# Float32 hybrid encoder step on one core: the blocks of the split activations move from a stride of 292 floats to 320, all starting at 32 modulo 256 bytes

## The chip, the cores and the metric

One Trainium2 chip, one of its cores. The metric is the device time of one execution in microseconds (us); the kernel before was run three times (median 2174.95 us) and once more under the hardware profiler.

## The reference

One layer of a streaming encoder for 256 prompt frames and 32 sample frames, with model width 2048, all in float32:

```python
x = x + 0.5 * swiglu(rmsnorm(x, norm_ffn1), w_ffn1_in, w_ffn1_out)   # 2048 -> 2 x 5504 -> 2048
y, state = mix(rmsnorm(x, norm_mix))   # h @ w_in, split among three head groups:
#   A: GLA linear attention, 4 heads, chunks of 64; B: differential attention, 4 heads;
#   C: cross-attention into 256 memory tokens (w_mem_kv); then concat @ w_o
x = x + y
x = x + 0.5 * swiglu(rmsnorm(x, norm_ffn2), w_ffn2_in, w_ffn2_out)
return rmsnorm(x, norm_final), state
# rmsnorm(x, g) = x * rsqrt(mean(x^2) + 1e-6) * g ; swiglu(x) = (silu(x @ gate) * (x @ up)) @ w_out
```

## The kernel before

**Layout.** Activations are kept transposed: `x_res` holds x as 16 blocks of 128 features (partitions) by NT = 288 tokens (free axis). In every large product the weights are the stationary operand of TensorE, in tiles of 128x128, and a block of 288 tokens is the moving operand; the output is a block of 128 output features by 288 tokens in PSUM.

**Split in two.** To keep float32 precision on TensorE's fast float32r path, each operand is split into a high and a low half (`split`, `gsplit`): hi is a copy rounded to float32r, lo is the rest. A product is three matmuls: weights-hi x moving-hi, weights-hi x moving-lo, weights-lo x moving-hi. The split activations are `uh`, `ul` (input of the FFNs and of the mixer, 16 blocks), `hh`, `hl` (the FFN's hidden activations, 22 blocks, named `hha`, `hhb`, ... for the two FFNs), `cdh`, `cdl` and `gch`, `gcl` (mixer outputs that go into w_o). Blocks of `uh`, `ul`, `hh`, `hl` lie NS = 292 floats apart, those of the last four NT = 288 floats apart.

**Weights.** All weights pass through one ordered list of chunks of mostly 128x1024 floats (4 k-blocks of 256 columns): a load into one of three `ws` buffers by the SP queue (L169), a split into `wh` on ScalarE (L102, the profile's ACT) and `wl` on VectorE (L90, DVE) into one of four buffers each, then the matmuls. `consume` hands out a chunk, splits three chunks ahead and loads three further. `gemm` gives a chunk 24 matmuls: first, for each of two column blocks and four k-blocks, wh with hi and wh with lo; then wl with hi. Four chunks make one output pair of 2x128 features from 16 k-blocks:

```python
                        if part == 0:
                            mm(o, wh[:, j, cs], xh, ci == 0 and j == 0, False)
                            mm(o, wh[:, j, cs], xl, False, False)
                        else:
                            mm(o, wl[:, j, cs], xh, False, ci == nchunk - 1 and j == nk - 1)
```

**Order.** The program order of each engine is written by hand: memory keys and values (w_mem_kv, where the weights are the moving operand with 512 columns and `mTh`, `mTl` the stationary one), FFN 1, mixer projection w_in, w_o, FFN 2. Between chunks `side()` takes small steps of four threads (attention heads, preparations).

**Normalisation.** The row scale R of rmsnorm is applied after the product. `prep_sq` sums squares into `acc`; `later_R` sums `acc` over the partitions with a matmul against ones and turns it into R in `rsq` (six instructions on VectorE and ScalarE); the outputs of each product are then multiplied by R through `Rb`. R has a tile of its own, R_ffn1, R_mix, R_ffn2 in one buffer. In the mixer, `glr` (16 rows x 288) is the low-rank gate input, of which the product has 16 columns only (`mglr`), and `wg2` its second weights; `mats` holds constants: a 128x128 block matrix `bones` of which only two columns are used (`bcols`), a mask `tri` and a row mask `smask`.

**Addresses.** Tiles of a pool lie behind one another in the order in which they are first used, each rounded up to 32 bytes. So in each partition `uh` starts at byte 20608 and `ul` at 39296 (both 128 modulo 256), `hh` at 150048 (32 modulo 256) and `hl` at 175744 (128). With a stride of 1168 bytes, which is 144 modulo 256, block k of `uh` and `ul` starts at 128 + 144k modulo 256, of `hh` at 32 + 144k. `cdh`, `cdl`, `gch`, `gcl` have a stride of 1152 bytes, so that their blocks start at 32 and 160 by turns. The weights buffers begin at byte 74016 and follow in steps of 4096; every 128-column block in them starts at 32 modulo 256.

Of the kernel before, what the change touches and what calls it, by code (L numbers as in the profile page):

```python
# [10 lines left out]
F32 = mybir.dt.float32  # L11
# [7 lines left out]

P = 128  # L20
NT = 288
NS = 292
D = 2048
KB = 16
NF = 43
# [9 lines left out]
G_MEM, G_F1, G_MQ, G_MIX, G_F2, G_FIN, G_BG, G_GO, G_DO, G_DQ, G_N = 0, 16, 32, 33, 49, 65, 81, 85, 87, 88, 89  # L35
# [5 lines left out]
def hybrid_step_kernel(  # L41
# [9 lines left out]
    pe, dve, act, sp = nc.tensor, nc.vector, nc.scalar, nc.sync  # L51
# [4 lines left out]
    const = pool("const")  # L56
# [10 lines left out]
    def c4(name):  # L67
        return c4p.tile([P, 1024], F32, tag="c4", name=name)
# [10 lines left out]
    def sq2(name):  # L79
        return sqp.tile([P, 2, NT], F32, tag="sq", name=name)  # L80
# [11 lines left out]
    def mul(out, a, b):  # L92
        dve.tensor_tensor(out, a, b, op=ALU.mult)  # L93
# [220 lines left out]
    ones = const.tile([P, P], F32, name="ones")  # L314
    dve.memset(ones, 1.0)
    x_res = const.tile([P, KB, NT], F32, name="x_res")
    uh = const.tile([P, KB, NS], F32R, name="uh")[:, :, :NT]
    ul = const.tile([P, KB, NS], F32R, name="ul")[:, :, :NT]
    acc = const.tile([P, NT], F32, name="acc")
    G = const.tile([P, G_N], F32, name="G")  # L320
    dkc = const.tile([P, 4, P], F32, name="dkc")
    dvc = const.tile([P, 512], F32, name="dvc")
    Bx = const.tile([P, 4, 384], F32, name="Bx")
    Bs = const.tile([P, 160], F32, name="Bs")
    lam = const.tile([P, 1], F32, name="lam")
    mkn = ft.tile([P, P], F32, name="mkn")
    gdk = const.tile([P, 64], F32, name="gdk")
    mats = const.tile([P, 544], F32, name="mats")
    bones, tri, smask = mats[:, 0:128], mats[:, 128:256], mats[:, 256:544]
    bcols = bones.rearrange("p (b c) -> p b c", c=64)[:, :, 0]  # L330

    def gcol(i):
        return G[:, i:i + 1]

    def rsq(out, src, n, rows=P, scale=1.0, tiles=None):

        w = src.shape[1]
        v, r, t = tiles or (sm(f"rs{k}")[:rows, :w] for k in range(3))
        dve.tensor_scalar(v, src, 1.0 / n, EPS, op0=ALU.mult, op1=ALU.add)
        act.activation(r, v, AF.Ln)  # L340
        act.activation(r, r, AF.Exp, scale=-0.5)
        mul(t, v, r)
        stt(t, t, -0.5 * scale, r, ALU.mult, ALU.mult)
        stt(out, t, 1.5 * scale, r, ALU.add, ALU.mult)

    def rsq_all(out, sums, v, n):

        ps = s1("sums")
        mm(ps[:, :NT], ones, sums)
        rsq(out, ps[:, :NT], n, tiles=(v, out, sums))  # L350


    T3 = (0, 128, 160)
# [20 lines left out]
        for b in (2 * i, 2 * i + 1):  # L374
            gsplit(uh[:, b, :], ul[:, b, :], x_res[:, b, :], gcol(g0 + b))

    Rt = {}

    def later_R(name):

        def f():
            R = const.tile([P, NT], F32, tag="R", name=f"R_{name}")
            rsq_all(R, acc, sq2("rw")[:, 0, :], float(D))
            fresh[0] = True
            Rt[0] = R
        t_main.add(f, f"R_{name}")

    def Rb(n):
        return Rt[0].unsqueeze(1).to_broadcast([P, n, NT])


    hp = fstack[0][1]
    mTh = hp.tile([P, 22, NS], F32R, tag="hh", name="mTh").rearrange("p a t -> p (a t)")[:, :4096]
    mTl = hp.tile([P, 22, NS], F32R, tag="hl", name="mTl").rearrange("p a t -> p (a t)")[:, :4096]
    mTh = mTh.rearrange("p (k m) -> p k m", m=256)
# [5 lines left out]
    tr(pt[:, :16], gmem)  # L401
    act.copy(G[:, :16], pt[:, :16])

# [132 lines left out]
    S = {}  # L536

    def lam_a():
        ld = S["ld"] = sq2("ld").rearrange("p a c -> p (a c)")[:, :256]
        sp.dma_start(ld, diff_lambda[0].rearrange("a d -> (a d)").unsqueeze(0).partition_broadcast(P))  # L540
        sp.dma_start(gdk, diff_k_norm.partition_broadcast(P))
        sp.dma_start(mats, c_mats[:, 128:672])

    def lam_b():
        l4 = S.pop("ld").rearrange("p (a b d) -> p a b d", a=2, b=2)
# [81 lines left out]
        dve.tensor_copy(Bx[:, :, 0:128], Bx[:, :, 256:384])  # L627

    def wg2_a():
        S["wg2"] = c4("wg2")[:16, :512]  # L630
        sp.dma_start(S["wg2"], w_gla_g2[0])

    def s0_a():
# [10 lines left out]
    def ffn(tag, mark, g_next, final=False):  # L644
# [8 lines left out]
        for half, (a, b) in enumerate(HALVES):  # L653
            hh = hp.tile([P, 22, NS], F32R, tag="hh", name=f"hh{tag}{half}")[:, :, :NT]
            hl = hp.tile([P, 22, NS], F32R, tag="hl", name=f"hl{tag}{half}")[:, :, :NT]
            f = a
# [49 lines left out]
    mxp = mstack.enter_context(tc.tile_pool(name="mxp", bufs=1))  # L706
# [16 lines left out]
        dve.memset(a, 0.0)  # L723
    dec = mxp.tile([P, 4, 5], F32, name="dec")
    junk = mxp.tile([P, P], F32, name="junk")
    glr = mxp.tile([16, NT], F32, name="glr")
    rsm = mxp.tile([P, 9], F32, name="rsm")
    rsd = mxp.tile([P, 18], F32, name="rsd")
    osum = mxp.tile([P, 18], F32, name="osum")
# [402 lines left out]
    for kind, c0, g in MIX:  # L1132
        if kind == "glr":
            ps = psm.tile([P, 2, 512], F32, tag="m", name="mglr")
            nk, (wh, wl) = consume()
            for j in range(nk):
                o = ps[:16, 0, :NT]
                mm(o, wh[:, j, :], uh[:, j, :], j == 0, False)
                mm(o, wh[:, j, :], ul[:, j, :], False, False)
                mm(o, wl[:, j, :], uh[:, j, :], False, j == nk - 1)  # L1140
            mul(glr, ps[:16, 0, :NT], Rt[0][:16, :])
            for f in (lambda: gla_z(0), lambda: gla_z(1), gla_g1, gla_g2):
                t_gla.add(f)
            t_gla.add(gla_g3, "E1")
            t_gla.add(gla_g4)
            side()
            continue
        ps = gemm(4, u)
        need("R_mix")
        pv = ps[:, :, :NT]  # L1150
        if kind in ("mq", "dq", "dk", "dv", "gk"):
            if g == 0:
                M[kind] = t4(kind)
            mul(M[kind][:, 2 * g:2 * g + 2, :], pv, Rb(2))
        if kind == "gr":
            if g % 2 == 0:
                M.setdefault("sgr", []).append(t4("sgr"))
            raw = M["sgr"][g // 2][:, 2 * (g % 2):2 * (g % 2) + 2, :]
            mul(raw, pv, Rb(2))
        elif kind == "gk" and g == 1:  # L1160
            for j in range(2):
                t_gla.add(lambda j=j: gla_k1(j))
                t_gla.add(lambda j=j: gla_k2(j), lag=1)
        elif kind == "mq" and g == 1:
            head_sums(t_mem, "mq", ones[:, 0:1], 128.0, 1, rsm, MS)
            t_mem.pipe([[(mem_a, 0), (mem_c, 2), (mem_b, 1), (mem_e, 0)], [(mem_n, 0)]], 5, "mem", lags=(1, 2))
        elif kind == "dq" and g == 1:
            head_sums(t_diff, "dq", bcols, 64.0, 2, rsd, DS)
        elif kind == "dk" and g == 1:
            t_diff.pipe([[(dk_b, 1), (dk_a, 0)]], 3)  # L1170
        elif kind == "dv" and g == 1:
            for t in range(3):
                t_diff.add(lambda t=t: dv_a(t), lag=1)
            t_diff.pipe([[(diff_a, 0), (diff_c, 2), (diff_b, 1), (diff_s, 0)], [(diff_e, 0)], [(diff_n, 0)]], 5,
                        lags=(1, 1, 2))
            t_diff.add(dv_out, lag=1)
            t_diff.add(od_a)
            for k in range(3):
                t_diff.add(lambda k=k: od_b(k), "diff" if k == 2 else None, lag=1)
        elif kind == "gq":  # L1180
            need("E1")
            raw = sq2("gqraw")
            mul(raw, pv, Rb(2))
            qe = M["GB"][:, 2 * g:2 * g + 2, :]
            stt(qe, raw, 128 ** -0.5, qe, ALU.mult, ALU.mult)
        elif kind == "gv":
            if g == 0:
                need("mem")
                need("diff")
                M["gvt"] = [c4(f"gvt{t}") for t in range(3)]  # L1190
            raw = M["gv", g] = tL("gvraw")[:, :2 * NT].rearrange("p (b t) -> p b t", t=NT)
            mul(raw, pv, Rb(2))

            def f0(g=g):
                if g:
                    gla_D(g - 1)
                gla_v(g)

            def f1(g=g):
                gla_A(g)  # L1200
                if g:
                    gla_E(g - 1)
            t_gla.add(f0, lag=1)
            if g == 0:
                for t in range(3):
                    t_gla.add(lambda t=t: gla_kdt(t), lag=1, after="diff")
                t_gla.add(silu_r, lag=0)
            t_gla.add(f1, lag=1)
            t_gla.add(lambda g=g: gla_B(g), lag=1)
            t_gla.add(lambda g=g: gla_C(g), lag=1)  # L1210
            if g == 3:
                t_gla.add(lambda: gla_D(3), delay=2)
                t_gla.add(lambda: gla_E(3), "gla")
        side()

    for half in range(2):
        if half == 1:
            need("gla")
        for g in range(8):
            if half == 0:  # L1220
                ps = gemm(2, lambda k: (cdh[:, k, :], cdl[:, k, :]))
            else:
                ps = gemm(2, lambda k: tuple(a[:, k % 4, :] for a in M["cat", k // 4]))
# [48 lines left out]
    ps = s1("yss")  # L1272
# [7 lines left out]
    for k, (hf, t, parts) in enumerate(((0, 0, 2), (0, 1, 1), (0, 2, 1), (1, 2, 1), (1, 0, 1), (1, 1, 1))):  # L1280
        rows = slice(0, P) if t < 2 else slice(96, P)
        dst = y_prompt[0, t * P:(t + 1) * P] if t < 2 else y_sample[0]
        n = 1024 // parts
# [66 lines left out]
```

## Time and profile before

| what | value |
|---|---|
| median of three runs (lowest, highest) | 2174.95 us (2172.83, 2175.52) |
| the profiled execution | 2173.12 us |
| its span, first to last instruction | 2171.3 us |
| TensorE matmuls (PE): busy, number | 2152.7 us, 16010 |
| VectorE (DVE) busy | 1116.0 us |
| ScalarE (ACT) busy | 867.2 us |
| bytes moved by DMA | 353.72 MB, mean 163 GB/s |
| granted TensorE clock, mean | 0.997 |

PE stands for TensorE's matmuls and PEld for its weight loads, which run beside the matmuls. A matmul's own duration overlaps with the next one's; the distance between two starts is what one costs. In the lists, a group is named output<-inputs by the program's tile names, with the number of instructions after the x.

### The profile page before, as it was taken

The numbers are of one execution on the slowest core, as the hardware profiler recorded it, in microseconds if no ns is written. First come the engines' busy times: TensorE is split into PE (matmuls) and PEld (weight loads), VectorE is DVE, ScalarE is ACT, GpSimd is POOL, SyncE is SP. The second block draws the span as 40 slices with busy tenths as digits, with TensorE's granted clock in tenths as the row PEclk, the third lists the DMA queues.
The fourth block names the chain that finished last, engine by engine and source line by source line (L and its number), as shares of the span: only waits on it lengthen the run. The fifth ranks groups of instructions, "written<-read, shape, count | busy, mean of one in ns | idle before, by whom it ended". The sixth has DMA issues, their size and how long they took to land.

```text
span 2171.3 us, 37498 instructions
## 1 busy us (share of the span) xinstructions
PE 2152.7 (99%) x16010; PEld 2119.4 (98%) x16010; DVE 1116.0 (51%) x1315; ACT 867.2 (40%) x1117; POOL 0.7 (0%) x6
## 2 busy tenths in 40 slices
PE   8999999999999999999999999999999999999997
PEld 6999999999999999999999899999999999999997
DVE  6754444444554455554664666554444445444453
ACT  6643333333333344433444344333333333333433
POOL 0000000000000000000000000000000000000000
PEclk9999999999999999999999999999999999999999
DMA  7556555555555545554445345555555555555453
GB/s 257 165 177 199 169 169 176 161 168 168 164 163 172 164 153 169 174 161 121 120 138 151 114 152 166 165 164 170 168 164 162 164 175 156 171 169 165 154 162 117
DMA packets 351028, 353.72 MB, mean 163 GB/s; under 512 B 13889, under 2 KB 342717, under 8 KB 350861
## 3 DMA queue, kind: packets, MB, share of 16 engines
q1 hardware_dynamic: 350860, 351.32, 53.2%
q8 instruction: 125, 2.05, 0.4%
q14 instruction: 43, 0.34, 0.0%
HBM read 345.55 MB, written 5.64 MB: 162 GB/s over the span
## 4 chain that ended last, share of the span: by engine, by line
PE 99%; DMA 0%; ACT 0%; DVE 0%; SPq 0%; ACTq 0%; issue 0%; DVEq 0%
PE m L83 92%; PE mm L83 2%; PE go L83 1%; PE xt L87 0%; PE gKo L83 0%; PE mglr L83 0%; PE do L83 0%; PE mo L83 0%; DMA mem<-in_mem_prompt_dram 0%; PE gKe L83 0%; PE msc L83 0%; PE dsc L83 0%; PE mt L87 0%; PE sums L83 0%; PE yt L87 0%; PE hs_dq L83 0%
## 5 line engine op out<-in xcount | busy, mean ns | idle before, releaser
L90 DVE TENSOR_TENSOR wl<-ws,wh 128x1024 fp32r<-128x1024 f32 (+2 forms) x665 | 781.8, 1190 | 678.6 <-ACT wh L102 648.1
L102 ACT CAST wh<-ws 128x1024 fp32r<-128x1024 f32 (+2 forms) x665 | 665.9, 1020 | 668.2 <-PE m L83 534.5
L83 PE MATMUL m<-uh,wh 128*128 128x288 f32 x3392 | 916.5, 296 | 0.0
L83 PE MATMUL m<-ul,wh 128*128 128x288 f32 x3392 | 911.1, 295 | 0.0
L83 PEld LDWEIGHTS m<-uh,wh 128*128 128x128 f32 x3392 | 638.5, 188 | 3.8 <-issue 2.9
L83 PEld LDWEIGHTS m<-ul,wh 128*128 128x128 f32 x3392 | 639.0, 188 | 0.2
L83 PE MATMUL m<-uh,wl 128*128 128x288 f32 x3392 | 517.7, 295 | 0.0
L83 PEld LDWEIGHTS m<-uh,wl 128*128 128x128 f32 x3392 | 473.5, 188 | 0.0
L83 PE MATMUL m<-hhb,wh 128*128 128x288 f32 x688 | 186.2, 296 | 0.0
L83 PE MATMUL m<-hla,wh 128*128 128x288 f32 x688 | 185.8, 296 | 0.0
L83 PE MATMUL m<-hlb,wh 128*128 128x288 f32 x688 | 185.7, 296 | 0.0
L83 PE MATMUL m<-hha,wh 128*128 128x288 f32 x688 | 185.7, 295 | 0.0
L83 PEld LDWEIGHTS m<-hlb,wh 128*128 128x128 f32 x688 | 129.9, 189 | 0.0
L83 PEld LDWEIGHTS m<-hla,wh 128*128 128x128 f32 x688 | 129.8, 189 | 0.0
L83 PEld LDWEIGHTS m<-hha,wh 128*128 128x128 f32 x688 | 129.3, 188 | 0.0
L83 PEld LDWEIGHTS m<-hhb,wh 128*128 128x128 f32 x688 | 129.3, 188 | 0.0
L83 PE MATMUL m<-hha,wl 128*128 128x288 f32 x688 | 106.7, 295 | 0.0
L83 PE MATMUL m<-hhb,wl 128*128 128x288 f32 x688 | 106.6, 295 | 0.0
L83 PEld LDWEIGHTS m<-hha,wl 128*128 128x128 f32 x688 | 96.6, 188 | 0.0
L83 PEld LDWEIGHTS m<-hhb,wl 128*128 128x128 f32 x688 | 96.6, 188 | 0.0
L665 ACT ACTIVATE gs_b<-gs_b 128x576 f32<-128x576 f32 (+1 forms) x22 | 14.8, 674 | 84.8 <-DVE gs_b L93 84.8
L102 ACT CAST hhb<-hm_b 128x576 fp32r<-128x576 f32 (+1 forms) x22 | 14.6, 663 | 83.4 <-DVE hm_b L93 83.4
(286 smaller groups left out, 1195.9 us busy)
## 6 DMA issues: line engine op xcount, KB each, us to landing
ws<-in_w_ffn_in_dram SPq DMA_DIRECT2D x336, 512.0 KB, 4.5
ws<-in_w_ffn_out_dram SPq DMA_DIRECT2D x160, 512.0 KB, 3.6
ws<-in_w_in_dram SPq DMA_DIRECT2D x80, 512.0 KB, 3.7
ws<-in_w_o_dram SPq DMA_DIRECT2D x32, 512.0 KB, 3.7
ws<-in_w_mem_kv_dram SPq DMA_DIRECT2D x16, 512.0 KB, 4.8
ws<-in_w_ffn_out_dram SPq DMA_DIRECT2D x16, 256.0 KB, 2.8
ws<-in_w_ffn_in_dram SPq DMA_DIRECT2D x16, 256.0 KB, 3.9
x<-in_x_prompt_dram SPq DMA_DIRECT2D x4, 512.0 KB, 7.3
```

The lines of the kernel that those rows point to most:

```text
L83: pe.matmul(out, lhsT, rhs, start=start, stop=stop)
L90: dve.tensor_tensor(out, a, b, op=op)
L102: act.copy(hi, src)
L665: act.activation(gs, gs, AF.Silu)
```

## The change

NS becomes 320, so that the stride is 1280 bytes, five times 256. `G` and `lam` are moved ahead of `uh`, which puts `uh` at byte 21024 and `ul` at 41504, both 32 modulo 256; with 20480 and 28160 bytes per tile, `hh` (152096) and `hl` (180256) come to 32 modulo 256 too, and so does the start of the weights buffers (76064). Each block of `uh`, `ul`, `hh`, `hl` then starts at 32 modulo 256 bytes. `mTh` and `mTl`, which use the buffers of `hh` and `hl`, do so as well.

To make room, R is written over `acc`, with the second half of the scratch tile as the temporary that `acc` was; `mats` shrinks from 544 to 442 floats by loading two columns of `bones` alone, with two DMAs in place of one; `glr` moves into the unused part of the `wg2` buffer.

```diff
-NS = 292
+NS = 320
...
     x_res = const.tile([P, KB, NT], F32, name="x_res")
+    G = const.tile([P, G_N], F32, name="G")
+    lam = const.tile([P, 1], F32, name="lam")
     uh = const.tile([P, KB, NS], F32R, name="uh")[:, :, :NT]
     ul = const.tile([P, KB, NS], F32R, name="ul")[:, :, :NT]
     acc = const.tile([P, NT], F32, name="acc")
-    G = const.tile([P, G_N], F32, name="G")
...
-    lam = const.tile([P, 1], F32, name="lam")
...
-    mats = const.tile([P, 544], F32, name="mats")
-    bones, tri, smask = mats[:, 0:128], mats[:, 128:256], mats[:, 256:544]
-    bcols = bones.rearrange("p (b c) -> p b c", c=64)[:, :, 0]
+    mats = const.tile([P, 442], F32, name="mats")
+    bcols, tri, smask = mats[:, 0:2], mats[:, 2:130], mats[:, 130:418]
...
-    def rsq_all(out, sums, v, n):
+    def rsq_all(out, sums, v, n, t=None):
...
-        rsq(out, ps[:, :NT], n, tiles=(v, out, sums))
+        rsq(out, ps[:, :NT], n, tiles=(v, out, sums if t is None else t))
...
-            R = const.tile([P, NT], F32, tag="R", name=f"R_{name}")
-            rsq_all(R, acc, sq2("rw")[:, 0, :], float(D))
+            w = sq2("rw")
+            rsq_all(acc, acc, w[:, 0, :], float(D), w[:, 1, :])
             fresh[0] = True
-            Rt[0] = R
...
     def Rb(n):
-        return Rt[0].unsqueeze(1).to_broadcast([P, n, NT])
+        return acc.unsqueeze(1).to_broadcast([P, n, NT])
...
-        sp.dma_start(mats, c_mats[:, 128:672])
+        sp.dma_start(mats[:, 0:2], c_mats[:, 191:193])
+        sp.dma_start(mats[:, 2:418], c_mats[:, 256:672])
...
-        S["wg2"] = c4("wg2")[:16, :512]
+        a = c4("wg2")
+        S["wg2"], S["glr"] = a[:16, :512], a[:16, 512:512 + NT]
...
-    glr = mxp.tile([16, NT], F32, name="glr")
+    glr = S["glr"]
...
-            mul(glr, ps[:16, 0, :NT], Rt[0][:16, :])
+            mul(glr, ps[:16, 0, :NT], acc[:16, :])
```

More of the change, by code (lines that the diff above doesn't have):

```diff
@@ L375, in prep_u @@
             gsplit(uh[:, b, :], ul[:, b, :], x_res[:, b, :], gcol(g0 + b))
-    Rt = {}
     def later_R(name):
         def f():
-            R = const.tile([P, NT], F32, tag="R", name=f"R_{name}")
-            rsq_all(R, acc, sq2("rw")[:, 0, :], float(D))
+            w = sq2("rw")
+            rsq_all(acc, acc, w[:, 0, :], float(D), w[:, 1, :])
             fresh[0] = True
-            Rt[0] = R
         t_main.add(f, f"R_{name}")
     def Rb(n):
-        return Rt[0].unsqueeze(1).to_broadcast([P, n, NT])
+        return acc.unsqueeze(1).to_broadcast([P, n, NT])
     hp = fstack[0][1]
```

## The prediction

> **What bounds the kernel now.** I read the page first (busy shares, the chain), then the chain in order of time, then the start times of single matmuls on TensorE.
>
> ```profile
> span 2171.3 us, 37498 instructions
> ...
> PE 2152.7 (99%) x16010; PEld 2119.4 (98%) x16010; DVE 1116.0 (51%) x1315; ACT 867.2 (40%) x1117; POOL 0.7 (0%) x6
> ...
> PE 99%; DMA 0%; ACT 0%; DVE 0%; SPq 0%; ACTq 0%; issue 0%; DVEq 0%
> ```
>
> TensorE is the chain: 99% of it. ACT and DVE are busy 40% and 51%, so only TensorE's own pace or a new wait on it can move the end. "Busy" says nothing about pace, since matmuls overlap (296 ns each in the groups below). The pace is the distance from one start to the next, and the chain in order of time has it:
>
> ```profile
> 29.49 5.54 PE mm L83 x24
> ...
> 294.96 601.10 PE m L83 x4536
> ...
> 1075.53 6.26 PE mglr L83 x48
> ```
>
> Columns: start, length, what, how many. 4536 matmuls of 288 columns, all in the first FFN, run without a gap in 601.10 us: 132.5 ns each. Set beside the memory stage (the first row: 512 columns, 5.54/24 = 230.8 ns), the difference is 98.3 ns over 224 columns, 0.439 ns a column; so 288 columns cost 126.4, and 6.1 ns come on top of each matmul.
>
> How many matmuls read a tile whose stride changes (`uh`, `ul`, `hh`, `hl`; the stage letters a and b stand behind the last two):
>
> ```profile
> L83 PE MATMUL m<-uh,wh 128*128 128x288 f32 x3392 | 916.5, 296 | 0.0
> ...
> L83 PE MATMUL m<-uh,wl 128*128 128x288 f32 x3392 | 517.7, 295 | 0.0
> L83 PE MATMUL m<-hhb,wh 128*128 128x288 f32 x688 | 186.2, 296 | 0.0
> ...
> L83 PE MATMUL m<-hhb,wl 128*128 128x288 f32 x688 | 106.6, 295 | 0.0
> ```
>
> Three groups of 3392 (`uh` and `ul` with wh, `uh` with wl) and six of 688 (`hh`, `hl` with wh and `hh` with wl, in two FFNs), of each the first and the last shown: 14304. (Each mean of the wl rows is 295 too; only overlap makes their busy sums small.) One ns on each of these is 14.3 us, 0.66% of the span. So a change of 0.2%, about what a measurement of this kernel can tell from no change, is 0.3 ns per matmul.
>
> **Does the start of a block matter at all, and what is it worth at 32?** The kernel before answers this by itself, because its blocks start at different places modulo 256 bytes. The gate's halves `gch`, `gcl` in the second part of w_o have blocks 1152 bytes apart, starting by turns at 32 and at 160; their order is hi, lo of block 0 (32), hi, lo of block 1 (160), and so on. TensorE's timeline (start, length, what):
>
> ```profile
> 1305.72 0.29 PE L83 MATMUL m<-gch,wh 128*128 128x288 f32 x1
> 1305.85 0.29 PE L83 MATMUL m<-gcl,wh 128*128 128x288 f32 x1
> 1305.98 0.30 PE L83 MATMUL m<-gch,wh 128*128 128x288 f32 x1
> 1306.12 0.29 PE L83 MATMUL m<-gcl,wh 128*128 128x288 f32 x1
> 1306.25 0.29 PE L83 MATMUL m<-gch,wh 128*128 128x288 f32 x1
> 1306.38 0.29 PE L83 MATMUL m<-gcl,wh 128*128 128x288 f32 x1
> 1306.51 0.30 PE L83 MATMUL m<-gch,wh 128*128 128x288 f32 x1
> 1306.65 0.29 PE L83 MATMUL m<-gcl,wh 128*128 128x288 f32 x1
> 1306.79 0.29 PE L83 MATMUL m<-gch,wh 128*128 128x288 f32 x1
> ```
>
> The two pairs at 32 take 1305.72 to 1305.98 and 1306.25 to 1306.51, 0.52 us for four matmuls: 130 ns each. The two pairs at 160 take 0.27 and 0.28: 137.5 ns each. Same weights buffers, same PSUM, same shape; so the place of the moving block is worth some 7 ns between two places. In `uh` and `ul` block 10 is the one where both start at 32, and block 11 behind it starts at 176:
>
> ```profile
> 511.76 0.29 PE L83 MATMUL m<-uh,wh 128*128 128x288 f32 x1
> 511.89 0.29 PE L83 MATMUL m<-ul,wh 128*128 128x288 f32 x1
> 512.02 0.30 PE L83 MATMUL m<-uh,wh 128*128 128x288 f32 x1
> 512.16 0.30 PE L83 MATMUL m<-ul,wh 128*128 128x288 f32 x1
> 512.30 0.29 PE L83 MATMUL m<-uh,wh 128*128 128x288 f32 x1
> ```
>
> Again 0.26 us for the pair at 32 (130 ns each) and 0.28 for the other (140). Against that, `hh` block 0 starts at 32 while its partner `hl` starts at 128:
>
> ```profile
> 387.00 0.30 PE L83 MATMUL m<-hha,wh 128*128 128x288 f32 x1
> 387.14 0.30 PE L83 MATMUL m<-hla,wh 128*128 128x288 f32 x1
> 387.27 0.29 PE L83 MATMUL m<-hha,wh 128*128 128x288 f32 x1
> ```
>
> Here the one at 32 takes 0.14 us, the pair 0.27 (135 each). So the start of one block does not fix its pace; neighbours count too, and nothing in this trace has 32 everywhere.
>
> **The change part by part.**
>
> Stride 292 to 320 floats. Before, block k of `uh`/`ul` starts at 128 + 144k modulo 256, so all sixteen multiples of 16 occur and 132.5 ns is the mean over them; after it, every moving block starts at 32, as every weights block does already (their buffers start at byte 74016, 32 modulo 256, and move on by 512). For the new common pace there are bounds on both sides. The lower one is the `mglr` group of the chain, 48 matmuls with the same moving blocks but weights of 16 columns instead of 128:
>
> ```profile
> 1075.29 0.38 PE L83 MATMUL mglr<-uh,wh 128*16 128x288 f32 x1
> 1075.50 0.29 PE L83 MATMUL mglr<-ul,wh 128*16 128x288 f32 x1
> ```
>
> 6.26/48 is 130.4 ns each; its first one took 0.21 us, some 0.08 more than the rest, and without that the mean is 128.7. Almost no weights are read there, so a pace much under it would need a gain that does not lie in the meeting of the two reads. The upper one is 135 (the `hh` row). I take 131: the rows in which hi and lo both start at 32 are nearest to the new layout and give 130; I add 1 because the `hh` row is worse and a third of the matmuls (those with wl) have no such pair. That is 132.5 − 131 = 1.5 ns x 14304 = 21.5 us saved. The matmuls of `cdh`, `cdl`, `gch` and `gcl` keep stride 288 and gain nothing.
>
> Does the rest of the kernel follow? Each weights chunk gives TensorE 24 matmuls, 3.18 us, and would give 3.14. Its split takes 1.19 us on DVE, the busier of the two engines that do it (first row, by the page's groups), and the loads wait for DVE to free a buffer, not for bandwidth (second, by the list of waits):
>
> ```profile
> L90 DVE TENSOR_TENSOR wl<-ws,wh 128x1024 fp32r<-128x1024 f32 (+2 forms) x665 | 781.8, 1190 | 678.6 <-ACT wh L102 648.1
> ```
>
> ```profile
> SPq L169 <- DVE wl L90: 1706.3, 636, 9.3
> ```
>
> With 636 waits on DVE, SP stands ready; a TensorE faster by 1% is still fed. If that cover went, a late split would stop TensorE; at 51% DVE it is far off.
>
> R now lives in `acc`. Instructions are the same in number and shape; only targets differ.
>
> ```profile
> L93 DVE TENSOR_TENSOR acc<-rw,R_ffn x2: 458/458/459, 73.5 to 1337.5; 128x288 f32<-128x288 f32 x2
> ```
>
> Ln writes `acc` only after DVE has read the sums out of PSUM into `rw`, and that read waits for the matmul that reads `acc`. The next stage's first sum of squares overwrites R; all readers of R are DVE instructions issued earlier on the same queue. So no wait is added; were one added, it would be one step of 0.46 us, three times, behind 96 matmuls (four chunks, 12.7 us) that run before R is needed. Cost 0, at most 1.4 us.
>
> `mats` is loaded by two DMAs instead of one:
>
> ```profile
> L542 SPq DMA_DIRECT2D mats<-in_c_mats_dram x1: 432/432/432, 114.2 to 114.2; - x1
> ```
>
> One more issue of about 0.43 us on SP, with a weights load behind it; loads run several chunks of 3.2 us ahead, so it is hidden; `mats` is first used in the mixer, a whole FFN later. `bcols` becomes two adjacent columns instead of two 64 apart, in a handful of small matmuls: nothing. `glr` moves into the `wg2` buffer, which was held until the same two steps anyway: 0. The halves of the memory stage that are weights there move from 128 to 32 in one of two tiles: by the row of 5.54 us for 24 matmuls, 3 ns on each of its 192 would be 0.6 us.
>
> Sum: the profiled execution took 2173.1 us (span 2171.3 and 1.8 around it); minus 21.5 is 2151.6. The median of the runs shown, 2174.95, is 1.9 above that execution, so I say 2152.
>
> **A rule beside these rows.** The trace has 130 against 137.5 ns by place of the moving block. The Trainium skill, "TensorE: Matmul & The Clock Gate", Part 2 (Step-by-step: what each phase is for), says that the moving operand and the weights come through two independent read ports, and that loading the next weights takes no read bandwidth from the running matmul. By that the place could not matter and the sum would stay 2173.1; the rows of `gch` do not bear it out in full.
>
> **Rivals.**
>
> Nothing happens. The mean over a mixture may be what it costs in any layout: the loss is then not from places but from a history that restarts elsewhere. For it: the 512-column matmuls of the memory stage always read blocks at 32 and still pay 0.439 ns a column. Against it: 130 against 137.5. Time: 2171 to 2177.
>
> A common place locks into a good meeting. Every matmul would then have the pace that `mglr` bounds, 128.5: 4.0 x 14304 = 57 us, 2116. For it: 130 in both clean pairs with bad neighbours around them. Against it: the memory stage again.
>
> A common place locks into a bad meeting, the one on the other side: moving block and the next weights block both start at 32, read at the same moment, and collide in each matmul, where before only one in sixteen did. For it: 0.14 us for `hh` at 32. At 134 ns it costs 1.5 x 14304 = 21.5 us: 2194.6. It decides from 132.8 ns on. Against it: all six gaps quoted with both halves at 32 say 130.
>
> **How the numbers follow.** Forecast (130 to 132.2 ns, 2137 to 2169): 0.45. Good lock: 0.16. Nothing: 0.13. Bad lock: 0.26. So faster 0.61, same 0.13, slower 0.26. As cases of both signs hold much, the range runs from the good lock's 2116 to the bad lock's 2195; about half of the good lock's chance and a third of the bad lock's lie outside it, not quite 2 in 10.
>
> **What would show it.** The long row of the chain with 4536 matmuls should last 4536 x 131 = 594 us; starts within `uh`/`ul` should be even from block to block, where they now run from 0.26 to 0.28 a pair. `gch` pairs should stay as they are. A row with 608 us or more is the bad lock; gaps before m on PE with a DVE or DMA as releaser would mean that a cover failed. Equal starts at 132.5 would say that places never mattered to the mean.

## The result, and the profile after

The changed kernel takes 2162.3 us (four runs, 2162.21 to 2163.05) against 2174.1 us before (2172.83 to 2175.52): ratio 0.9946, 95% interval 0.9929 to 0.9964, 11.7 us faster. The span of the profiled execution fell from 2171.3 to 2160.5 us, by 10.8.

The page of the changed kernel has the same engines, shares and instruction counts:

```profile
span 2160.5 us, 37498 instructions
...
PE 2141.6 (99%) x16010; PEld 2108.3 (98%) x16010; DVE 1115.8 (52%) x1315; ACT 866.3 (40%) x1117; POOL 0.7 (0%) x6
...
PE 99%; DMA 0%; ACT 0%; DVE 0%; SPq 0%; ACTq 0%; issue 0%; DVEq 0%
```

TensorE lost 11.1 us of busy time and the span 10.8; DVE and ACT lost 0.2 and 0.9. The chain in order of time says where (start, length, what):

```profile
29.92 5.47 PE mm L83 x24
...
293.96 597.24 PE m L83 x4536
...
947.05 6.32 PE m L83 x48
...
1070.00 6.26 PE mglr L83 x48
...
2031.94 16.59 PE m L83 x126
...
2118.18 16.59 PE m L83 x126
```

The long piece of FFN 1 takes 597.24/4536 = 131.67 ns a matmul where it took 132.52. The last six output products of FFN 2, of which the first and last stand here, take 16.59/126 = 131.67 ns each, the mixer piece 6.32/48 = 131.7: the blocks at 32 now have the same pace in all three stages. Between single matmuls of `uh` and `ul`:

```profile
508.67 0.30 PE L83 MATMUL m<-uh,wh 128*128 128x288 f32 x1
508.81 0.29 PE L83 MATMUL m<-ul,wh 128*128 128x288 f32 x1
508.94 0.29 PE L83 MATMUL m<-uh,wh 128*128 128x288 f32 x1
509.07 0.29 PE L83 MATMUL m<-ul,wh 128*128 128x288 f32 x1
509.20 0.30 PE L83 MATMUL m<-uh,wh 128*128 128x288 f32 x1
509.33 0.29 PE L83 MATMUL m<-ul,wh 128*128 128x288 f32 x1
509.46 0.29 PE L83 MATMUL m<-uh,wh 128*128 128x288 f32 x1
509.59 0.29 PE L83 MATMUL m<-ul,wh 128*128 128x288 f32 x1
509.72 0.30 PE L83 MATMUL m<-uh,wh 128*128 128x288 f32 x1
```

The pairs take 0.27, 0.26, 0.26 and 0.26 us; before they ran from 0.26 to 0.28. Note that single gaps still differ (0.14 and 0.13 in the first pair) though every block and every weights tile starts at the same place. The starts are printed to 0.01 us, so a gap of 0.13 or a pair of 0.26 cannot tell 130 from 131.67 ns: a gap is not the pace.

### The profile page after: what moved, and what is told of

It reads as the page before. It is cut to its first block, busy times and chain, and to the rows that moved or that the text cites. A ratio compares the mean times of both kernels' runs of the same rounds, so it can differ in the third digit from the quotient of the medians.

```text
span 2160.5 us, 37498 instructions
## 1 busy us (share of the span) xinstructions
PE 2141.6 (99%) x16010; PEld 2108.3 (98%) x16010; DVE 1115.8 (52%) x1315; ACT 866.3 (40%) x1117; POOL 0.7 (0%) x6
## 4 chain that ended last, share of the span: by engine, by line
PE 99%; DMA 0%; ACT 0%; DVE 0%; SPq 0%; ACTq 0%; issue 0%; DVEq 0%
PE m L83 92%; PE mm L83 2%; PE go L83 1%; PE xt L87 0%; PE gKo L83 0%; PE mglr L83 0%; PE do L83 0%; DMA mem<-in_mem_prompt_dram 0%; PE mo L83 0%; PE gKe L83 0%; PE msc L83 0%; PE dsc L83 0%; PE mt L87 0%; PE sums L83 0%; PE yt L87 0%; PE hs_dq L83 0%
```

## The experiments

Every kernel here is the changed kernel with one edit. Paces are piece lengths over matmul counts, as above. "Distance" is the start of the moving blocks less that of the weights, modulo 256 bytes: 0 in the changed kernel (32 and 32).

**The stride alone put back.**

```diff
-NS = 320
+NS = 292
```

> The changed kernel with the stride put back to 292 floats: merged buffers, moved tiles and split DMA stay. If the gain is all from the stride, the blocks start at all multiples of 16 again, the pace of the long FFN 1 piece is back at 132.5 ns a matmul and the time is that of before (2172 to 2176 us). Rival: the merged buffers carry part of it; then the pace is 132.5 but the time is under 2170, or over 2178 if they cost.

Measured: 2175.9 us against 2172.7, ratio 1.0014 (1.0005 to 1.0023). The long piece of FFN 1:

```profile
296.30 601.63 PE m L83 x4536
```

132.63 ns. So the merged buffers, the moved tiles and the second DMA gain nothing; the stride is the whole gain. The kernel is even slower than before by 3.2 us. Of the 2.8 us by which its profiled execution is longer (spans 2174.1 and 2171.3), the pieces `m` of the chain hold 1.8 (2004.6 against 2002.8 us in total), and 0.9 passed before the second piece of the memory stage (14.37 against 13.44 us), where the first load took longer (5.84 against 5.35). That `uh` and `ul` now start at 32 + 144k instead of 128 + 144k may be the reason for the first; it was not tested.

**Other common starts.** `uh`, `ul`, `hh` and `hl` get 256 bytes of slack, and each stage takes its own offset into it, in bytes after 32, for hi and lo. An FFN works through its hidden features in two halves, `a0` and `a1` in FFN 1, `b0` and `b1` in FFN 2. An excerpt of the edit for the first of two kernels; the second has other numbers:

```diff
+    ur = const.tile([P, 2 * KB * NS + 64], F32R, name="u")
+    PH = {G_F1: (128, 128), G_MIX: (4, 4), G_F2: (64, 64)}
+    HPH = {"a0": (192, 192), "a1": (32, 32), "b0": (96, 96), "b1": (16, 16)}
...
+        return raw[:, o:o + n * NS].rearrange("p (k t) -> p k t", t=NS)[:, :, :NT]
```

> Stride 320, but the common start of the moving blocks (weights always start at 32 modulo 256) differs by stage: FFN 1 input 160, mixer 36, FFN 2 input 96, first FFN's hidden halves 224 and 64, second FFN's 128 and 48. If only evenness matters (every block at the same place), each stage keeps 131.7 ns a matmul and the span stays 2160 us. If the place matters, alone or relative to the weights, the stages differ: from the rows of before, 160 should be the worst with 134 to 137 ns and 64 and 224 near 131; FFN 1 input at 135 would add 4128 x 3.3 = 14 us. Start 36 is off the multiples of 16: a reader by 16-byte lines would need one line more per block, 0.4 to 1.7 ns.

> The same with other starts: FFN 1 input 176, mixer 144, FFN 2 input 40, first FFN's hidden halves 192 and 0, second FFN's 80 and 112. Evenness alone: 131.7 ns everywhere. Place: 176 near 134, 144 near 130.7, 0, 80 and 192 near 132, 112 near 133.5, as the means over the mixed neighbours of before.

Measured: 2178.8 and 2168.7 us (one execution each). From the chain of the first of them, asked for one stage at a time (FFN 1 input at 160, its hidden halves at 224 and 64, then FFN 2's hidden half at 128):

```profile
499.92 260.14 PE m L83 x1951
...
359.93 130.13 PE m L83 x976
...
769.93 120.13 PE m L83 x901
...
1624.88 125.21 PE m L83 x951
```

133.3, 133.3, 133.3 and 131.7 ns. And from the second (FFN 1 input at 176, its first hidden half at 192, FFN 2's first hidden half at 80, FFN 2 input at 40):

```profile
499.97 240.11 PE m L83 x1847
...
359.98 120.13 PE m L83 x901
...
1614.92 125.19 PE m L83 x963
...
1339.98 260.13 PE m L83 x1951
```

130.0, 133.3, 130.0 and 133.3 ns. The stages not shown: 132.2 for the FFN 2 input at 96, 131.7 for a hidden half at 48, 133.3 at 0 and 131.2 at 112. Evenness alone is refuted: common starts give 130.0 to 133.3 ns. So is reading the pace of a start off mixed neighbours: 160 was expected worst and 64 and 224 near the best, and all three came out at the same 133.3; 176, expected near 134, held 130.0. Pieces of the mixer at 36, off the multiples of 16, were slower still:

```profile
958.35 6.51 PE m L83 x48
```

135.6 ns, against 131.7 in the mixer piece of the changed kernel; other pieces of the same mixer took 3.20 us for 24, 133.3 ns. Start 40 is off those multiples too and had 133.3.

**The weights alone moved by 64 bytes.** A pad moves the weights to 96, and with them every tile that lies behind it; an offset of 192 brings `hh` and `hl` back to 32, so that all moving blocks stay at 32 (an excerpt of the edit):

```diff
     mats = const.tile([P, 442], F32, name="mats")
+    pad = const.tile([P, 16], F32, name="pad")
+    dve.memset(pad[:, 0:1], 0.0)
...
+    HPH = {"a0": (192, 192), "a1": (192, 192), "b0": (192, 192), "b1": (192, 192)}
```

> All moving blocks stay at 32 modulo 256, the weights buffers alone are moved on by 64 bytes, to 96. If the pace hangs on the distance from the weights' start, it becomes that of a moving block at 224 beside weights at 32 (the first hidden half of FFN 1 in the kernel sent with this one), whatever that is. If it hangs on the moving block's own place, or on evenness alone, it stays 131.7 ns and the span 2160 us. The gate's blocks keep their distance (0 and 128) while both move by 64: 133.3 ns on the mean as before if the distance decides.

Measured: 2185.5 us (one execution), 23 us over the changed kernel.

```profile
296.59 604.80 PE m L83 x4536
```

133.33 ns: the pace of a block at 224 beside weights at 32, the same distance of 192. The moving blocks had not moved, so their own place is not what sets the pace; their distance from the weights fits both kernels.

**Both moved by 64 bytes, distance kept at 0** (the pad, and an offset of 64 for `uh`, `ul`).

> Moving blocks and weights both moved on by 64 bytes, to 96, distance 0 as in the changed kernel. Distance: every stage at 131.7 ns, 2161 to 2164 us. Place of either one alone: the moving blocks at 96 took 131.9 ns beside weights at 32 and the weights at 96 took 133.3 beside moving blocks at 32; the time then leaves 2164 upward, to 2185.

Measured: 2162.2 us (2161.95 to 2162.36), ratio to before 0.9948 (0.9933 to 0.9962), the changed kernel's time to 0.2 us, with the same pace:

```profile
293.98 597.24 PE m L83 x4536
```

Together the two say: distance 0 gives 131.67 ns at either place, and the weights moved alone give 133.33. The pad is the same in both, so what else it moves is not the cause.

**All blocks at 80, distance 48**, the best start of the sweep together with 176:

> All moving blocks at 80 modulo 256 beside weights at 32, the distance 48 that gave 130.0 ns in one hidden half of the sweep. If the distance alone sets the pace, every changed matmul costs 130.0 instead of 131.7 ns, the long FFN 1 piece lasts 590 us, and the time is 1.66 x 14304 = 24 us under the changed kernel's: 2138 to 2140. Rival, the pace belongs to that stage (its place in the buffer, its 22 blocks): the FFN inputs keep 131 to 133 ns and the time stays at 2160 or above.

Measured: 2166.0 us (2164.48 to 2166.63), ratio 0.9964 (0.9950 to 0.9977). It is slower than the changed kernel, against the distance theory as it stood. The chain:

```profile
291.18 601.02 PE m L83 x4536
...
2034.86 16.70 PE m L83 x126
2052.21 16.39 PE m L83 x126
```

The long piece runs at 132.5 ns, not 130.0. Two output products of the same hidden half, with the same moving tiles and the same distance, run one at 132.5 and the next at 130.1. So one distance can hold two paces; between these two products the stream is broken by transposes.

**Distance 48 again, both 64 bytes further** (the pad; moving blocks at 144, weights at 96).

> The same distance 48 with both moved on by 64 bytes: moving blocks at 144, weights at 96. Distance: 130.0 ns everywhere, 2138 to 2140 us. Place of the moving block alone: 144, which took 134.3 ns in the mixer of the second sweep, makes this kernel slower than before, 14304 x 2 = 29 us over 2173.

Measured: 2143.0 us median, but in two groups, 2142.1 to 2143.0 (three) and 2154.0 to 2154.1 (two); ratio 0.9877 (0.9854 to 0.9900). The profile fell on one of the slower ones:

```profile
292.15 601.02 PE m L83 x4536
...
2025.06 16.39 PE m L83 x126
```

Here FFN 1 holds 132.5 ns and FFN 2 130.1. The step between the groups, 11 us, is what FFN 1's long piece would gain at 130.0: 2.5 x 4536 = 11.3 us. That the faster executions are those in which it does was not seen, since no profile fell on one. The theory of the moving block's own place (29 us slower than before) is refuted once more. But distance does not tell all either: at the same distance, all five executions here lie 10 us or more below all five of the kernel at 80 and 32, and in the profiles a stretch of 5334 matmuls of FFN 2 took 693.42 us here and 706.75 there. Whether the place that both operands share decides between the two paces, or something else that differs between the kernels, was not separated.

**The missing starts, and unequal halves.**

> The starts still missing, and pairs whose halves differ. FFN 1 input 208, first FFN's hidden halves 16 and 240, mixer 80; FFN 2 input hi 80 and lo 176, second FFN's hidden halves hi 176 and lo 80, then hi 80 and lo 48. If each matmul's cost follows from its own distance to the next weights, pairs of 80 and 176 cost 130.1 ns and the pair of 80 and 48 lies at two thirds of 130.0 and one third of 131.7, 130.6. If the neighbour's place counts too, the mixed pairs come out elsewhere, 131 to 135. For 208, 16 and 240 the distance theory has no number beforehand beyond the 130 to 133.3 seen so far; the mixer at 80 should be at 130.0.

Measured: 2161.9 us (one execution). Starts 208, 16 and 240 gave 131.4, 132.0 and 133.3 ns. The unequal pairs, hi 80 with lo 176 in FFN 2's input, hi 176 with lo 80 and hi 80 with lo 48 in its two hidden halves, as the chain has them:

```profile
1744.92 255.09 PE m L83 x1936
...
1609.95 125.08 PE m L83 x950
...
2030.98 16.67 PE m L83 x126
```

131.8, 131.7 and 132.3 ns, where adding up each matmul's own pace gave 130.1, 130.1 and 130.6. So the neighbour counts too: paces of starts do not add.

**All blocks at 176, distance 144.**

> All moving blocks at 176 beside weights at 32, the distance 144, which held 130.0 or about 131.0 ns for long stretches of the second sweep and nothing above. If the distance sets which paces a stream can hold, each stage here holds one of 130.0 to 131.1 ns, and the time is 14304 x 0.6 to 1.7 = 8 to 24 us under the changed kernel's 2162: 2138 to 2154, below before in every run. Rival: a pace belongs to the stage, not to the distance; then paces of 132 ns and more appear in stages that did not have this start in the sweep.

Measured: 2150.8 us (2148.64 to 2153.21), ratio 0.9892 (0.9876 to 0.9909): faster than before in every run, and 11.5 us faster than the changed kernel.

```profile
291.87 594.72 PE m L83 x4536
...
2057.97 16.52 PE m L83 x126
2075.14 16.38 PE m L83 x126
```

131.1 ns in the long piece, 131.1 and 130.0 in two neighbouring products. Two paces again, both below 131.67, as expected.

**Interruptions.** The kernel at start 80 with one transpose, whose result nothing uses, ahead of each output product of the FFNs (an excerpt of the edit):

```diff
             for g in range(8):
+                tr(s1("brk")[:, :P], x_res[:, 2 * g, 0:P])
                 ps = gemm(len(kparts(b - a)), lambda k: (hh[:, k, :], hl[:, k, :]))
```

> The kernel with all blocks at 80 (distance 48), which held 130.0 ns in some stretches and 132.5 in others, with one extra 128x128 transpose on TensorE ahead of each of the 32 output products of the two FFNs; its result is used by nothing. If a stream keeps the pace that it falls into after an interruption, the long stretches at 132.5 break up: pieces of 130.0 and 132.5 ns from one output product to the next, no other paces, and the FFN input that follows the last break of a half holds the pace of the piece before it. If the stage fixes the pace, all pieces of the first FFN stay at 132.5. The breaks themselves cost some 0.2 us each, 6 us.

Measured: 2155.9 us (one execution), 10 us faster than without the extra work. FFN 1 up to the first break, three neighbouring products, and the stretch behind the last break of its first half:

```profile
294.03 57.25 PE m L83 x432
...
403.22 17.17 PE m L83 x132
420.50 17.49 PE m L83 x132
438.10 17.18 PE m L83 x132
...
472.65 279.25 PE m L83 x2148
```

132.5 ns up to the first break, then 130.1, 132.5 and 130.2, and 130.0 for the 2148 matmuls behind the last one, in a stage that without breaks held 132.5 throughout. Here a stream keeps the pace that it has after an interruption. One break costs 0.11 us (403.22 + 17.17 to 420.50).

> The kernel with the 32 extra transposes again, timed in rounds. Its one look had 26 of the 32 output products at 130.0 ns and six at 132.5. If each interruption draws a pace anew and mostly the good one, the mean pace is some 130.5 ns in every execution, the 32 breaks cost 32 x 0.11 = 3.5 us, and the time is 2162 less 1.2 x 14304 = 17 us plus 3.5, about 2149 with a spread of some 8 us, in any case under the 2164 to 2167 of the same kernel without breaks. If the one look was luck, the median returns to 2164 or more.

Measured: 2154.0 us (2152.72 to 2159.65), ratio 0.9922 (0.9909 to 0.9936). Below the 2164 of the kernel without breaks in every run, and 5 us above the 2149 expected. Its profile again has 132.5 ns in the fifth output product of FFN 1:

```profile
418.62 17.49 PE m L83 x132
```

In FFN 1 the same five of its 16 products ran at 132.5 in both executions; in FFN 2 they were others. So a fresh even draw at each break does not fit.

## Why the prediction was right, and where it was off

**That places matter, and the stride is the whole effect: right.** The kernel with the stride put back loses the gain; the one with the weights moved alone loses twice as much. That place could not matter, as the prediction drew it from the Trainium skill's two independent read ports ("TensorE: Matmul & The Clock Gate", Part 2, Step-by-step: what each phase is for), is not borne out by this stream: 64 bytes in the weights' address cost 133.33 − 131.67 = 1.66 ns a matmul.

**The size of the term: half.** The prediction took 1.5 ns x 14304 = 21.5 us. Measured are 132.52 − 131.67 = 0.85 ns, 12.2 us by that product and 10.8 in the span. The step that failed is "the rows in which hi and lo both start at 32 are nearest to the new layout and give 130". In the uniform layout the pair at 32 takes 0.26 or 0.27, and the mean is 131.67: a pair read as 0.26 from starts printed to 0.01 us never told 130 from 131.67. Nor does a gap in a mixed row stand for its block alone. The sweep shows how poor such readings are: by them 160 and 64 lay 3 ns or more apart, and as common starts both take 133.3; block 11 at 176 was read at 140, and 176 as a common start took 130.0 or 131.1.

**The lower bound from `mglr`, 128.7: misread.** The prediction took the slow first gap, 1075.29 to 1075.50, off a piece of the chain that starts only at 1075.53 and so does not hold it. From the second start, 1075.50, to the last, 1081.49, are 46 gaps: 130.2 ns each. No pace under 130.0 was seen in any long stretch of `m` in any kernel.

**The good lock (2116) did not come, and its price was too high.** It rests on the 128.5 of that reading. With 130.0 the gain is at most 2.5 ns x 14304 = 36 us, which gives 2137; the lowest execution of any kernel here took 2142.1. Stretches at 130.0 ns do exist, at distances 48 and 144; at distance 0 none was seen. **The bad lock** did not come at distance 0 either, but at 192, where the kernel took 2185.5 us, 11 over before. The prediction's rivals expected a common place to lock into one meeting; at distances 0 and 192 each profile held one pace, at 48 and 144 two. They put the start "at the same moment" as the worst case, and the worst ones were distances 8, 32, 128, 160, 192, 208 and 224 (all 133.3) and, in pieces of the mixer, 4 (135.6) and 112 (134.2).

**The covers held.** Neither before nor after does a product `m`, or the load of its weights, stand in the list of waits with DVE or a DMA as releaser. SP still waits for DVE to free its buffers, not for bandwidth, and the last step of R and each of the two `mats` loads cost what the old ones did:

```profile
SPq L169 <- DVE wl L90: 1692.9, 635, 9.3
```

```profile
L538 SPq DMA_DIRECT2D mats<-in_c_mats_dram x1: 432/432/432, 114.2 to 114.2; - x1
L539 SPq DMA_DIRECT2D mats<-in_c_mats_dram x1: 430/430/430, 114.7 to 114.7; - x1
```

```profile
L99 DVE SCALAR_TENSOR_TENSOR acc<-rw,acc x3: 457/459/460, 74.7 to 1332.3; 128x288 f32<-128x288 f32 x3
```

The second load is the 0.43 us on SP that was counted; the last step of R is the 0.46 us that it was. `gch` was to stay as it was, and its pairs still alternate:

```profile
1299.57 0.29 PE L83 MATMUL m<-gch,wh 128*128 128x288 f32 x1
1299.70 0.29 PE L83 MATMUL m<-gcl,wh 128*128 128x288 f32 x1
1299.83 0.30 PE L83 MATMUL m<-gch,wh 128*128 128x288 f32 x1
1299.97 0.29 PE L83 MATMUL m<-gcl,wh 128*128 128x288 f32 x1
1300.10 0.29 PE L83 MATMUL m<-gch,wh 128*128 128x288 f32 x1
```

0.26 for the pair at 32 and 0.27 for the one at 160.

**What stays open.** That it is the moving read and the read of the next weights that meet is the reading that fits the distance; the experiments show that the distance counts, not by what mechanism. At distance 48 moving both operands by 64 bytes changed the time as well, which distance alone does not explain. Which pace of two a stream falls into after a break, and why one kernel falls differently from one execution to the next, was not settled.

## What to carry to other kernels

In a stream of matmuls at full pace, the distance of the moving operand's start from the weights' start modulo 256 bytes is worth up to 2.5% here (130.0 to 133.3 ns): give all blocks a common one by padding the stride, and choose it by a sweep of whole stages, several starts in one kernel, not by single gaps of a trace whose blocks start at different places. Then look whether the pace holds after interruptions and over several executions: start 176 (2150.8 us) gained 23 us and spread over 5, distance 48 gained 8 us with the blocks at 80 and 31 with both operands 64 bytes further.

## What the runs showed of the hardware that was not expected

- Many steady paces lie at few values: 130.0, 131.67, 132.5 and 133.33 ns are 156, 158, 159 and 160 times 0.8333. Stretches of 4536 matmuls held 131.67 (distance 0), 132.5 (48) and 133.33 (192). Other stretches lie between: 131.1 at distance 144, 131.4 at 176, 132.0 at 240. Why was not looked into.
- One distance can hold two paces (130.0 and 132.5 at 48; 130.0 and 131.1 at 144), and a break of 0.11 us can move the stream from one to the other. At distance 0 only 131.67 was seen in long stretches, and the runs of those two kernels agree within 0.9 and 0.4 us.
- 32 transposes whose result nothing uses made a kernel 12 us faster (2166.0 to 2154.0 in medians).
